# A hybrid attention decoder block: the partition swaps of the rotary tiles issued from ScalarE's queue

## The chip, the cores and the metric

The kernel runs on 1 core of one Trainium2 chip. The metric is the device time of one execution in microseconds (us). The engines are named as the profile names them: PE is TensorE (matmuls and transposes), DVE is VectorE, ACT is ScalarE, POOL is GpSimd, SP is SyncE, which does no arithmetic here and issues the DMAs. SPq and ACTq are the sequencers of SP and ACT, where a DMA instruction is issued. Each engine works through its own instructions strictly in order.

## The reference, cut to what matters

One decoder layer on 512 tokens of width 1024, all in float32: an RMS norm, one projection `h @ w_in` into queries, keys and values of two attention branches and two gates, a rotary embedding of the queries and keys, branch A (dilated window attention, 8 heads of 64), branch B (an indexer scores all keys, the best 128 of each row are kept, 8 query heads share one key head), a gated merge, an output projection, and a SwiGLU feed-forward part with a final norm. The rotary embedding is the part that the change touches:

```python
def rope(z, pos):
    half = z.shape[-1] // 2
    ...
    z1, z2 = z32[..., :half], z32[..., half:]
    return jnp.concatenate([z1 * cos - z2 * sin, z2 * cos + z1 * sin], axis=-1).astype(z.dtype)
```

Each head's 64 numbers are two halves of 32, and each half needs the other one.

## The kernel before

Every float32 operand of a matmul is split into a rounded part and a remainder (`hi`, `lo`), and a product is three matmuls (L201, L202, L203, in `mm3`). Weights come by DMA from SP into `raw` tiles (L153, five buffers), ACT copies them to `whi` (L172), and POOL or DVE makes the remainder `wlo` (L164), which also frees the `raw` buffer for the next load.

In the first quarter the kernel makes, slot by slot, the transposed queries and keys (`slot_parts`: 128 features by 512 tokens in PSUM). In that layout a head's two halves lie in different partitions, 32 apart. `rope_T` therefore copies the slot from PSUM to an SBUF tile on ACT (also named `raw`, L488, two buffers, shared tag `rp`), and swaps neighbouring blocks of 32 partitions with SBUF-to-SBUF DMAs into a tile `sw` (L491): four DMAs of 64 KB for a slot of 128 rows, two for the one with 64. `sw` is one of 39 rotating buffers (tag `k2`) that queries, keys and many other tiles share. DVE then multiplies `raw` by the cosines (L495), `sw` by the signed sines (L498), and adds (L499); ACT and DVE (L422, L426), or ACT and POOL (L441 to L447), split the sum `z` for the score matmuls. There are 13 such slots: 4 pairs of heads of branch A with 2 slots each, 4 query slots of branch B, and its keys (64 rows).

All this is laid under the attention steps of branch A. In each step (`attn_step`) two blocks go through scores on PE (L613), a masked maximum on DVE (L678), `exp` on ACT (L679), a reciprocal on DVE (L683), the normalisation on POOL (L684), transposes on PE (L693), and the split of these into `pth` on ACT (L697) and `ptl` on DVE (L698); products with the values give `y` (L708, L710), drained through `low` on ACT (L712) and added on DVE (L714). Before those, the indexer's dot products go through `relu` on ACT (L861) and a running sum `score` on DVE (L864, L866). The search for the best 128 (L629, L634, then L640 to L647) runs on DVE between all that and has to be done before branch B.

The order on PE is written out by hand. On the other engines a scheduler picks, by priority, among the instructions that are ready in its own model of time. The attention step stands at a higher priority (a lower level) than the projections under which the rotary tiles are made:

```python
        with level(2):
            tiles = qk_units([(h.q, h.k, h.half, b) for h, b in units], "sc") if units else []
            ...
        fill(us)
    def fill(us):
        debt[0] += us
        with level(3):
            while queue and debt[0] > 0:
                run_part()
```

Every DMA of the kernel is issued from SP, and ACT's queue holds no DMA.

Of the kernel before, what the change touches and what calls it, by code (L numbers as in the profile page):

```python
# [38 lines left out]
def hybrid_block(ctx: ExitStack, tc: tile.TileContext, x, norm_mix, w_in, w_up_a, w_up_b, w_out,  # L39
                 norm_ffn, w_gate, w_up, w_down, norm_final, c_rope, c_ropeT, c_mask, out):  # L40
    nc = tc.nc
# [25 lines left out]
    def k2(dt=F32, name="k2"):  # L67
        return kp.tile([P, 512], dt, tag="k2", bufs=K2, name=name)
# [261 lines left out]
    def defer(n, fn):  # L330

        if MAN[0]:
            later.append([n, fn])
        else:
            fn()
# [149 lines left out]
    def rope_T(p_, rows, then):  # L485

        raw, sw, z = kp.tile([P, 512], F32, tag="rp", bufs=2, name="raw"), k2(name="sw"), k2(name="z")
        nc.scalar.activation(raw, p_, AF.Copy)  # L488
        for i in range(rows // 32):
            o = 32 * (i ^ 1)  # L490
            nc.sync.dma_start(sw[32 * i:32 * i + 32, :], raw[o:o + 32, :])  # L491
        r = slice(0, rows)

        def straight():
            (nc.vector if RT1 else nc.gpsimd).tensor_tensor(z[r, :], raw[r, :], ropeT[r, 0, :], op=ALU.mult)  # L495

        def crossed():
            (nc.vector if RT2 else nc.gpsimd).tensor_tensor(sw[r, :], sw[r, :], ropeT[r, 1, :], op=ALU.mult)  # L498
            (nc.vector if RT3 else nc.gpsimd).tensor_tensor(z[r, :], z[r, :], sw[r, :], op=ALU.add)  # L499
            defer(1, lambda: then(z))  # L500
        defer(1, straight)
        defer(3, crossed)
        return raw
# [22 lines left out]
    def mqa_parts(res):  # L526

        ws = [stream(win, [(QB + 256 * c, 256)]) for c in range(2)] + [stream(win, [(KB, 128)], per=4)]

        def done_q(i, p_):  # L530
            rope_T(p_, P, lambda z: res.__setitem__(1 + i, queries(z, f"qB{i}")))

        def done_kv(p_):
            kv.append(rope_T(p_, HD, lambda z: res.__setitem__(0, key_twice(z, "kB"))))

        def turn_v():
            t_ = acc("vT")
            for b in range(NB):
                nc.tensor.transpose(t_[:, b * HD:(b + 1) * HD], kv[0][HALF[1], b * P:(b + 1) * P], ident[HALF[1], HALF[1]])
            v = vb()  # L540
            for b in range(NB):
                src = t_[:, b * HD:(b + 1) * HD]
                nc.scalar.activation(v[:, b, 0:64], src, AF.Copy, scale=rs1[:, b:b + 1])
                nc.vector.scalar_tensor_tensor(v[:, b, 64:128], src, rs1[:, b:b + 1],
                                               v[:, b, 0:64].bitcast(F32), op0=ALU.mult, op1=ALU.subtract)
        kv = []
        return ([slot_parts(ws[2], 0, done_kv)] +
                [slot_parts(ws[i // 2], i % 2, lambda p_, i=i: done_q(i, p_)) for i in range(4)], [(0.43, turn_v)], ws)
# [20 lines left out]
    def qka_parts(pr):  # L569
        get_w = stream(win, [(QA + P * pr, P), (KA + P * pr, P)])  # L570
        qkA[pr] = {}

        def done(m, p_):
            rope_T(p_, P, lambda z: qkA[pr].__setitem__(m, (keys if m else queries)(z, f"qk{m}A{pr}")))
        return [slot_parts(get_w, m, lambda p_, m=m: done(m, p_)) for m in range(2)], get_w
# [475 lines left out]
    for b in range(NB):  # L1051
        v = None
        for h in range(2):
            for f in range(NF - LAST, NF):
                mm3(po[b, h], (actT[f][0][:, b * P:(b + 1) * P], actT[f][1][:, b * P:(b + 1) * P]), W[f, h], False, f == NF - 1)
            o = x1[b][h]
# [53 lines left out]
```

## Time and profile before

| | us |
|---|---|
| median of 3 runs (lowest to highest) | 774.34 (773.42 to 774.81) |
| the profiled execution, its own time | 774.55 |
| its span, from the first to the last instruction | 772.8 |
| PE busy in the span | 744.1 |
| DVE busy | 435.6 |
| ACT busy | 352.6 |
| POOL busy | 281.4 |
| granted TensorE clock, as a share of full speed | 0.993 |

Busy times are means over stages that differ much: the swaps are issued from 50 to 226 us, and what counts is which engine the others wait for in that stretch. DMA-issuing instructions are not counted as busy on the engine that issues them. Matmul durations overlap, so that a stretch in which PE is 100% busy can still hold short waits.

### The profile page before, as it was taken

To read this page: it belongs to the slowest core of one execution; us is meant where nothing else is said; L and a number is where in the kernel's file an instruction comes from. 1 tells how busy PE (TensorE), PEld (TensorE's weight loads), DVE (VectorE), ACT (ScalarE), POOL (GpSimd) and SP (SyncE) were. 2 spreads that over 40 slices of the span, in tenths; PEclk is the share of its full clock that TensorE was granted. 3 is DMA by queue.
4 is the path that set the end of the run, shared out by engine and by line. 5 is a ranking of instruction groups with operands and counts; after the bars stand their busy time and mean duration, and the time that the engine had idled before them with its cause. 6 is when DMAs were issued, how large, how long until landed. Compare 5 with 4: busy or idle time off the path is not lost.

```text
span 772.8 us, 10634 instructions
## 1 busy us (share of the span) xinstructions
PE 744.1 (96%) x3621; PEld 625.2 (81%) x3621; DVE 435.6 (56%) x910; ACT 352.6 (46%) x722; POOL 281.4 (36%) x263
## 2 busy tenths in 40 slices
PE   8988998988999999999999999999999999999995
PEld 7977887886888888888887888888888888888884
DVE  5789989997766557765334344344433343222235
ACT  7366566655666667533425333333333333121233
POOL 2653656645545455422121222222222222222223
PEclk9999999999999999999999999999999999999999
DMA  8352433322432221533232332233223333323202
GB/s 278 80 137 54 102 91 88 89 76 69 117 88 70 73 66 55 176 112 107 82 106 59 109 103 88 83 109 109 84 85 105 109 101 90 105 86 109 83 14 109
DMA packets 68502, 74.53 MB, mean 96 GB/s; under 512 B 5392, under 2 KB 55584, under 8 KB 68448
## 3 DMA queue, kind: packets, MB, share of 16 engines
q1 hardware_dynamic: 68448, 73.86, 32.7%
q8 instruction: 28, 0.46, 0.2%
q14 instruction: 26, 0.21, 0.1%
HBM read 68.46 MB, written 2.10 MB: 91 GB/s over the span
## 4 chain that ended last, share of the span: by engine, by line
PE 82%; DVE 10%; ACT 3%; issue 2%; DMA 1%; SPq 0%; POOL 0%; ACTq 0%; DVEq 0%; POOLq 0%
PE o L202 5%; PE u L203 5%; PE o L203 5%; PE u L202 5%; PE u L201 5%; PE o L201 5%; PE g L203 5%; PE g L202 5%; PE g L201 5%; PE gate L201 3%; PE gate L202 3%; PE gate L203 3%; PE x L203 2%; PE x L201 2%; PE x L202 2%
## 5 line engine op out<-in xcount | busy, mean ns | idle before, releaser
L164 POOL TENSOR_TENSOR wlo<-raw,whi 128x512 fp32r<-128x512 f32 (+1 forms) x156 | 206.1, 1331 | 386.6 <-ACT whi L172 376.4
L172 ACT ACTIVATE whi<-raw 128x512 fp32r<-128x512 f32 (+1 forms) x242 | 149.6, 625 | 240.1 <-PE u L203 70.9
L164 DVE TENSOR_TENSOR wlo<-raw,whi 128x512 fp32r<-128x512 f32 x86 | 71.9, 836 | 128.3 <-ACT whi L172 127.8
L201 PE MATMUL g<-h2h,whi 128*128 128x512 f32 x176 | 68.7, 390 | 0.0
L203 PE MATMUL g<-h2l,whi 128*128 128x512 f32 x176 | 68.7, 390 | 0.0
L202 PE MATMUL g<-h2h,wlo 128*128 128x512 f32 x176 | 68.6, 390 | 0.0
L201 PE MATMUL u<-h2h,whi 128*128 128x512 f32 x176 | 68.5, 389 | 0.0
L202 PE MATMUL u<-h2h,wlo 128*128 128x512 f32 x176 | 68.5, 389 | 0.0
L203 PE MATMUL u<-h2l,whi 128*128 128x512 f32 x176 | 68.5, 389 | 0.0
L201 PE MATMUL o<-whi,ah 128*128 128x512 f32 x176 | 68.5, 389 | 0.0
L202 PE MATMUL o<-whi,al 128*128 128x512 f32 x176 | 68.5, 389 | 0.0
L203 PE MATMUL o<-wlo,ah 128*128 128x512 f32 x176 | 68.5, 389 | 0.0
L684 POOL TENSOR_SCALAR sm<-sm,st 128x256 f32<-128x256 f32 (+3 forms) x64 | 40.0, 632 | 62.4 <-DVE st L683 52.1
L201 PE MATMUL gate<-hTh,whi 128*128 128x512 f32 x128 | 51.6, 403 | 0.0
L203 PE MATMUL gate<-hTl,whi 128*128 128x512 f32 x128 | 50.2, 392 | 0.0
L202 PE MATMUL gate<-hTh,wlo 128*128 128x512 f32 x128 | 50.1, 391 | 0.0
L679 ACT ACTIVATE sm<-sm,st 128x256 f32<-128x256 f32 (+3 forms) x64 | 35.6, 557 | 23.3 <-DVE st L678 23.1
L1025 DVE TENSOR_TENSOR u<-u,rb 128x512 f32<-128x512 f32 x22 | 15.2, 692 | 52.4 <-PE u L203 52.4
L201 PE MATMUL slot<-hTh,whi 128*128 128x512 f32 x104 | 41.7, 401 | 1.8 <-DVE va L563 1.1
L201 PE MATMUL proj<-whi,hTh 128*128 128x256 f32 (+1 forms) x128 | 38.4, 301 | 2.8 <-DVE va L563 1.2
L202 PE MATMUL slot<-hTh,wlo 128*128 128x512 f32 x104 | 40.8, 392 | 0.0
L203 PE MATMUL slot<-hTl,whi 128*128 128x512 f32 x104 | 40.7, 391 | 0.0
(268 smaller groups left out, 1627.0 us busy)
## 6 DMA issues: line engine op xcount, KB each, us to landing
raw<-in_w_in SPq DMA_DIRECT2D x54, 256.0 KB, 3.0
raw<-in_w_gate SPq DMA_DIRECT2D x44, 256.0 KB, 2.9
raw<-in_w_up SPq DMA_DIRECT2D x44, 256.0 KB, 2.9
raw<-in_w_down SPq DMA_DIRECT2D x44, 256.0 KB, 2.8
x<-in_x SPq DMA_DIRECT2D x16, 256.0 KB, 4.0
raw<-in_w_in SPq DMA_DIRECT2D x32, 128.0 KB, 2.5
raw<-in_w_out SPq DMA_DIRECT2D x16, 256.0 KB, 2.6
sw<-raw SPq DMA_DIRECT2D x50, 64.0 KB, 2.0
```

Of the source, the lines that this page charges most:

```text
L164: eng.tensor_tensor(lo, raw, hi.bitcast(F32), op=ALU.subtract)
L172: nc.scalar.activation(hi, raw, AF.Copy)
L201: nc.tensor.matmul(o, l[0], r[0], start=start, stop=False)
L202: nc.tensor.matmul(o, l[1], r[0], start=False, stop=False)
L203: nc.tensor.matmul(o, l[0], r[1], start=False, stop=stop)
L679: nc.scalar.activation(sm, sm, AF.Exp, bias=st[:, 0:1], scale=-1.0, accum_out=st[:, 1:2])
L684: nc.gpsimd.tensor_scalar(sm, sm, st[:, 2:3], 1.0, op0=ALU.mult, op1=ALU.mult)
L1025: nc.vector.tensor_tensor(u, p_, rb2, op=ALU.mult)
```

## The change

The swap DMAs of `rope_T` are issued from ACT's queue in place of SP's. Their number, sizes, sources and targets stay as they are: 12 slots with four and one with two, 50 in all.

```diff
--- before.py
+++ after.py
@@ -488,7 +488,7 @@
         nc.scalar.activation(raw, p_, AF.Copy)
         for i in range(rows // 32):
             o = 32 * (i ^ 1)
-            nc.sync.dma_start(sw[32 * i:32 * i + 32, :], raw[o:o + 32, :])
+            nc.scalar.dma_start(sw[32 * i:32 * i + 32, :], raw[o:o + 32, :])
         r = slice(0, rows)
 
         def straight():
```

## Rows read from the trace of the kernel before

**Rows 1.** Busy time of each engine in three stretches of the span (us from its start): the width, PE, PE's weight loads, DVE, ACT, POOL with their instructions, the granted clock, the DMA share and GB/s.

```profile
50.00:110.00 60.00, 55.95 (x303) 48.80 (x302) 58.54 (x137) 37.60 (x77) 29.67 (x25) 0.97 0.34 84
110.00:190.00 80.00, 71.76 (x385) 60.23 (x383) 74.80 (x191) 48.13 (x110) 46.27 (x42) 0.99 0.32 82
190.00:230.00 40.00, 40.00 (x198) 33.61 (x198) 26.05 (x61) 24.58 (x57) 21.82 (x22) 0.97 0.40 105
```

**Rows 2.** Issues on SP's queue, of the swaps (L491) and of the loads of `w_in` (L153): duration in ns (lowest, median, highest), and the first and last start in us. The last line is from the page's costliest groups: ACT's copies of weights, with their count, busy us, mean ns of one, and ACT's idle time before them.

```profile
L491 SPq DMA_DIRECT2D sw<-raw x50: 507/582/1610, 50.3 to 225.7; - x50
...
L153 SPq DMA_DIRECT2D raw<-in_w_in x94: 328/373/584, 2.4 to 252.2; - x94
...
L172 ACT ACTIVATE whi<-raw 128x512 fp32r<-128x512 f32 (+1 forms) x242 | 149.6, 625 | 240.1 <-PE u L203 70.9
```

**Rows 3.** What SP's queue waited for from 48 to 230 us: in total, times, longest (us).

```profile
SPq L153 <- POOL wlo L164: 92.2, 40, 14.7
SPq L491 <- ACT whi L172: 11.4, 4, 4.1
SPq L491 <- ACT raw L488: 10.7, 4, 4.9
...
SPq L491 <- PE pT L693: 0.3, 1, 0.3
```

**Rows 4.** The two instructions of DVE's timeline that waited for a swap to land; in brackets the idle time before them and what ended it.

```profile
193.47 0.69 DVE L498 TENSOR_TENSOR sw<-sw,ropeT 128x512 f32<-128x512 f32 x1 [2.32 <-DMA sw<-raw]
...
219.38 0.97 DVE L498 TENSOR_TENSOR sw<-sw,ropeT 128x512 f32<-128x512 f32 x1 [1.40 <-DMA sw<-raw]
```

**Rows 5.** Two pieces of the chain that ended last, where it runs over a swap (its issue, and its way from issue to landing): start and length in us.

```profile
109.56 0.86 SPq L491
...
110.47 2.08 DMA sw<-raw
```

**Rows 6.** The timeline around the first two rotary slots (start, length in us, engine, line, what): ACT, SP's queue and DVE.

```profile
49.66 0.60 ACT L488 ACTIVATE raw<-slot 128x512 f32<-128x512 f32 x1 [0.19 <-PE slot L203]
50.28 2.50 SPq L491 DMA_DIRECT2D sw<-raw  x4
50.35 1.09 ACT L861 ACTIVATE relu<-dots 128x512 f32<-128x512 f32 x2
...
51.55 0.48 DVE L864 TENSOR_SCALAR score<-relu,wis 128x512 f32<-128x512 f32 x1
...
53.26 2.18 DVE L866 SCALAR_TENSOR_TENSOR score<-relu,wis,score 128x512 f32<-128x512 f32 x2 [0.38 <-ACT relu L861]
...
61.80 0.60 ACT L488 ACTIVATE raw<-slot 128x512 f32<-128x512 f32 x1
62.29 0.87 ACT L861 ACTIVATE relu<-dots 128x384 f32<-128x384 f32 x2
...
63.26 0.42 DVE L864 TENSOR_SCALAR score<-relu,wis 128x384 f32<-128x384 f32 x1
```

**Rows 7.** The timeline around the third and fourth slot: ACT and DVE.

```profile
88.96 0.58 ACT L488 ACTIVATE raw<-slot 128x512 f32<-128x512 f32 x1
...
92.86 0.60 ACT L488 ACTIVATE raw<-slot 128x512 f32<-128x512 f32 x1 [0.73 <-PE slot L203]
...
93.87 0.59 ACT L697 ACTIVATE pth<-pT 128x512 fp32r<-128x512 f32 x1
...
94.65 0.67 DVE L698 TENSOR_TENSOR ptl<-pT,pth 128x512 fp32r<-128x512 f32 x1
...
97.94 1.29 ACT L422 ACTIVATE qk0A<-z 64x512 fp32r<-64x512 f32 x2 [2.74 <-DVE z L499]
```

**Rows 8.** The timeline around the fifth and sixth slot: ACT, SP's queue and DVE.

```profile
99.47 0.60 ACT L488 ACTIVATE raw<-slot 128x512 f32<-128x512 f32 x1 [0.24 <-ACT qk0A L422]
...
109.33 3.00 SPq L491 DMA_DIRECT2D sw<-raw  x4
...
112.55 0.57 ACT L488 ACTIVATE raw<-slot 128x512 f32<-128x512 f32 x1
...
114.08 0.42 DVE L698 TENSOR_TENSOR ptl<-pT,pth 128x256 fp32r<-128x256 f32 x1 [2.42 <-ACT pth L697]
...
117.44 1.29 ACT L422 ACTIVATE qk0A<-z 64x512 fp32r<-64x512 f32 x2 [1.93 <-DVE z L499]
```

**Rows 9.** The timeline around the seventh and eighth slot, and one row behind the ninth (the slot of 64 rows): ACT and DVE.

```profile
132.55 0.58 ACT L488 ACTIVATE raw<-slot 128x512 f32<-128x512 f32 x1
...
134.13 0.59 ACT L712 ACTIVATE low<-y 64x512 f32<-64x512 f32 x1
...
134.82 0.67 DVE L714 TENSOR_TENSOR A0y<-y,low 64x512 f32<-64x512 f32 x1
...
139.81 1.29 ACT L422 ACTIVATE qk0A<-z 64x512 fp32r<-64x512 f32 x2 [2.62 <-DVE z L499]
...
141.12 0.60 ACT L488 ACTIVATE raw<-slot 128x512 f32<-128x512 f32 x1
...
144.00 0.55 DVE L698 TENSOR_TENSOR ptl<-pT,pth 128x384 fp32r<-128x384 f32 x1
...
149.42 0.63 ACT L441 ACTIVATE qk1A30h<-z 64x512 fp32r<-64x512 f32 x1 [3.80 <-DVE z L499]
...
169.78 0.63 ACT L562 ACTIVATE va<-proj,rs 128x128 fp32r<-128x128 f32 x2 [3.99 <-DVE va L563]
```

## The prediction

> **What bounds the kernel now.** I read busy time by stretch first, since the swaps lie in the first 230 us alone. From 50 to 190 us two engines are full together: DVE is busy 58.54 of 60 and 74.80 of 80 us, PE 55.95 and 71.76. From 190 to 230 us PE alone is full, 40.00 of 40, and DVE has a third of its time free [rows 1]. ACT, which is to take the issues, is busy 37.60 of 60, 48.13 of 80 and 24.58 of 40 us: it has 22, 32 and 15 us free, 69 in all. Its mean load says little, though. What matters is what stands behind a swap in ACT's order, and how soon DVE wants it.
>
> Then the waits. SP's queue stands 92.2 us for POOL's `wlo`, which frees the buffers of the weight loads, and 11.4 + 10.7 us for ACT at the swaps themselves [rows 3]. So SP has time to spare, and the loads are paced by buffers, not by the swaps. DVE waits for a swap twice, 2.32 and 1.40 us [rows 4], both times after 190 us, where it isn't full. Swaps reach DVE in time as they are.
>
> **The change part by part.**
>
> *Taken from SP.* A swap's issue takes 582 ns in the median [rows 2]; 50 of them are 29.1 us of SP's queue. Worth nothing on the path: SP waits three times as long for POOL in this stretch [rows 3], and a load issued earlier would only find its buffer still taken. If that cover were gone, SP would give back at most its waits at the swaps, 22 us of its own queue.
>
> *Landing.* Size and partitions of the transfers stay, so I keep 2.1 us from issue to landing, as in the chain [rows 5]. A swap could start sooner where SP is late: the first goes out 0.02 us after its `raw` ends (49.66 + 0.60, then 50.28 [rows 6]), but the fifth only at 109.33, 9.3 us after 99.47 + 0.60 [rows 8]. On DVE that is worth nothing as long as DVE's order is full of other work there [rows 1].
>
> *Added to ACT.* No row shows an issue on ACT. Below, it could cost nothing (if it overlapped ACT's arithmetic); above, 1.61 us, the longest on SP [rows 2]. I take SP's median: same instruction, same shape. Four in a row take 4 x 0.582 = 2.33 us, and the first slot's four took 2.50 with their gaps [rows 6]; I use the middle, 2.41 a slot. While ACT's sequencer issues, it starts no activation, and before the first it must wait for its own `raw` to be written. The 1.61 us is one extreme in 50 and is no end of the range.
>
> Two queues would now issue at once, which no row here shows. SP's load issue takes 0.373 us [rows 2]. If issues excluded each other, a slot could meet one of them: 13 x 0.373 = 4.8 us on ACT, of which, in the ratio of path to issue below (8 of 29), 1.3 us would reach the end. I leave it out. The Trainium skill (Perfetto Trace Analysis, section "DMA Instruction — HWDGE (DVE, Sync)") says that an issuing sequencer locks a shared descriptor generator for exclusive use; by that rule the sum below would be 1.3 us longer, and the change would look worse.
>
> *What is queued behind.* I take each slot twice. "Right behind": the swaps follow `raw` at once, and all that ACT does next is 2.41 us late. "Behind what is ready": ACT first does the attention work (level 2 goes before level 3), and the swaps fall into its next idle gap.
>
> - Slot 1: DVE wants the first `relu` at 51.55. Right behind, ACT is free at 50.26 + 2.41 = 52.67 and that `relu` ends at 53.2: DVE 1.7 us late. Behind the two `relu` that end at 51.44, the swaps last till 53.85, and the third `relu` ends near 54.45 for a DVE instruction that began at 53.26: 1.2 [rows 6].
> - Slot 2: right behind, 62.40 + 2.41 + 0.45 = 65.3 for DVE's 63.26: 2.0. Behind: 0 [rows 6].
> - Slots 3 and 4: right behind, 89.54 + 2.41 = 91.95, then three `whi` of 0.625 till 93.8, `raw` till 94.4, swaps till 96.8, `whi` and `pth` (0.59) till 98.0, and DVE wanted `pth` at 94.65: 3.4. Behind, the fourth slot's swaps fit into the 2.74 us before 97.94: 0 [rows 2, 7].
> - Slot 5: its swap seems held until 109.33 for another reason (below). From there 2.41 us push the work before slot 6 by about 0.6, either way [rows 8].
> - Slot 6: DVE already stands 2.42 us for `pth` at 114.08, which comes right after `raw`. Right behind: 2.4. Behind: the gap of 1.93 before 117.44 is 0.5 short [rows 8].
> - Slot 7: `low` ends at 134.72, DVE wants it at 134.82. Right behind: 2.3. Behind: 0, in the 2.62 before 139.81 [rows 9].
> - Slot 8: swaps till 141.72 + 2.41 = 144.13, `whi` and a `pth` like the others till 145.2, DVE at 144.00: 1.2. Behind: 0, in the 3.80 before 149.42 [rows 2, 7, 9].
> - Slot 9, two swaps: 0, covered by the 3.99 before 169.78 [rows 9].
> - Slots 10 to 13: 0. DVE is a third free and PE full [rows 1]; what ACT hands over goes to the next attention step, 8 us on. Without that cover, up to 2.41 each, 9.6.
>
> Right behind: 1.7 + 2.0 + 3.4 + 0.6 + 2.4 + 2.3 + 1.2 = 13.6. Behind: 1.2 + 0.6 + 0.5 = 2.3. A stall of DVE before 190 us is not made good: DVE has 1.5 us free of 60 and 5.2 of 80 [rows 1], the top-128 search has to end before branch B, and PE, full from 190 us on, starts its last 580 us that much later. Each order has something for it (SP's swap goes 0.02 us after `raw` [rows 6]; the attention step's priority in the code is higher), so I take the middle, (13.6 + 2.3)/2 = 8.0 us. The profiled execution's own time is 774.55 (span 772.8 and 1.75 around it): 782.55. It lies 0.2 above the median of the runs, so the forecast for the median is 782.3.
>
> **The rivals.**
>
> *ACT is held by the target buffer.* `sw` comes from the shared pool of 39, and a swap must wait until its buffer's last reader is done. The fifth slot's swaps wait for PE [rows 3], and the chain runs from there over a swap issued at 109.56 [rows 5], 9.5 us after `raw` was written. On SP that wait stops loads that have time; on ACT it would stop `exp`, `pth` and `whi`. If the scheduler places that swap at its `raw`, the price is up to 9.3 us more on top of the sum: 782.3 + 9.3 = 791.6. It decides from about 2 us of such a hold on, the slack of the rows above. Against it: at the other slots that I looked at closely SP waited only for ACT, so the buffer was free, and the scheduler's own model knows when a buffer comes free.
>
> *The swaps disappear into ACT's gaps.* All "behind", with an issue shorter than on SP: below 1.5 us, about 774.3 to 775.8. For it: 69 us free on ACT for 29. Against: the rows of slots 1, 2, 4, 6 and 7 leave 0.1 to 0.6 us between ACT's result and DVE's use. The Trainium skill (DMA: Bandwidth & Descriptors, "Issuing engines are not separate DMA queues") says that issuing from several engines saves sequencer time only, usually small beside the transfer; by that rule the time would stay at 774.3. The trace half agrees: 0.582 us against 2.08.
>
> *Faster.* The chain runs at 109.56 from SP's swap over its landing at 112.55 to `raw` and on to the `pth` for which DVE stands 2.42 us [rows 5, 8]. If late swaps on SP are what holds ACT's `raw` there, an own queue ends that: the 2.42 us go, 774.3 - 2.4 = 771.9. It decides where slot 5's swap can start 2.4 us earlier. Against it: ACT had no idle time before that `raw` (its row shows none), so the landing may only coincide.
>
> **How the numbers follow.** A difference under 0.2% (1.55 us) is about what a measurement of this kernel can't tell from no change. Chances: the sum, +2.3 to +13.6, 0.57; held by the buffer, 0.15; into the gaps, 0.15; faster, 0.13. Slower is the first two, 0.72; same 0.15; faster 0.13. The range runs from 772.5 (half of the faster case stays out) to 790.0 (the sum's upper bound 787.9 and a little of a hold; most of the case held by the buffer, 0.12, stays out), so that about 0.19 is left out. The forecast's own range is 776.6 to 787.9.
>
> **What would show it.** In the changed profile ACTq issues 50 swaps of about 0.58 us, and SP's waits at L491 are gone. DVE's waits for ACT (`relu`, `pth`, `raw`, `low`) before 190 us grow by some 8 us, PE's busy time in 50 to 190 us stretches over 8 us more, and after 230 us nothing changes but the start. Wrong would be: an issue on ACT of clearly other length, the swaps all behind ACT's attention work, ACT idle at a swap for DVE or PE (the buffer), a scheduler that orders DVE's instructions anew so that gains and losses lie where no swap is, or a loss after 190 us, which I put at nothing.

## The result and the profile after

The changed kernel takes 783.78 us in the median of 4 runs (783.20 to 784.11); the kernel before, run beside it, takes 773.88 (773.18 to 774.81). The ratio is 1.0126, with a 95% interval of 1.0109 to 1.0144: 9.9 us slower, where the prediction said 782.3 and slower. Its profiled execution took 783.84 us, with a span of 781.8 and a granted clock of 0.989.

The number came out close. The way to it did not, and most of what follows is about that. First the busy time by stretch, in the columns and stretches of [rows 1]:

```profile
50.00:110.00 60.00, 54.62 (x292) 46.83 (x292) 56.55 (x120) 33.43 (x72) 23.16 (x21) 0.98 0.31 78
110.00:190.00 80.00, 67.31 (x356) 57.42 (x355) 76.68 (x190) 47.10 (x104) 47.08 (x41) 0.95 0.30 77
190.00:230.00 40.00, 40.00 (x195) 33.46 (x193) 27.50 (x63) 23.27 (x56) 23.04 (x23) 0.98 0.37 95
```

From 50 to 190 us PE is busy 121.9 us and was busy 127.7 [rows 1]; the granted clock from 110 to 190 us is 0.95 and was 0.99. DVE is as full as before and ACT a little emptier. From 190 us on PE is full again. The transposes of branch B's values (L539), at the end of the stretch with the swaps, start at 221.3 us before and 230.0 after. From there to the end the two kernels run in parallel: every later matmul is 8.8 to 9.0 us late.

Now the queues. The issues of the swaps on ACT (columns as in [rows 2]), and what SP waits for from 48 to 240 us:

```profile
L491 ACTq DMA_DIRECT2D sw<-raw x50: 513/602/1594, 52.3 to 236.4; - x50
DMA to landing us min/median/max: 1.9/2.1/3.4
```

```profile
SPq L153 <- POOL wlo L164: 157.6, 46, 16.8
```

An issue takes 0.602 us on ACT and took 0.582 on SP [rows 2]; landing stays at 2.1 us; SP's waits at L491 are gone, and its time went into waiting longer for POOL, 157.6 us against 92.2 in a window that ends 10 us earlier [rows 3]. So far everything is as predicted. Then DVE's waits from 48 to 190 us, first of the kernel before, then of the changed one (engine and line, what it waited for, total, times, longest):

```profile
DVE ptl L698 <- ACT pth L697: 2.6, 2, 2.4
DVE z L495 <- ACT raw L488: 1.2, 2, 1.0
DVE score L866 <- ACT relu L861: 0.7, 2, 0.4
DVE idx L426 <- ACT idx L422: 0.5, 1, 0.5
DVE va L563 <- ACT va L562: 0.4, 1, 0.4
```

```profile
DVE ptl L698 <- ACT pth L697: 2.3, 2, 1.7
DVE score L866 <- ACT relu L861: 1.2, 2, 0.7
DVE idx L426 <- ACT idx L422: 0.7, 1, 0.7
DVE st L683 <- ACT sm L679: 0.7, 1, 0.7
DVE z L495 <- issue: 0.6, 1, 0.6
DVE score L864 <- ACT relu L861: 0.5, 1, 0.5
```

DVE waits for ACT 5.4 us before and 5.4 after (2.3 + 1.2 + 0.7 + 0.7 + 0.5). The 8 us by which these waits were to grow are not there. PE's timeline shows where the time goes instead (start, length, line, what, and in brackets the idle time before it and what ended it):

```profile
83.81 0.47 PE L201 MATMUL slot<-hTh,whi 128*128 128x512 f32 x1 [2.72 <-DVE va L563]
...
140.99 0.79 PE L201 MATMUL gate<-hTh,whi 128*128 128x512 f32 x1 [3.26 <-DVE gate L590]
...
166.65 0.35 PE L201 MATMUL proj<-whi,hTh 128*128 128x256 f32 x1 [2.77 <-DVE gate L590]
...
187.05 0.47 PE L201 MATMUL slot<-hTh,whi 128*128 128x512 f32 x1 [3.02 <-DVE va L563]
```

PE stands 11.8 us at these four places, each time for DVE, and not for rotary work: DVE has not yet emptied a PSUM accumulator of the values (`va`, L563) or of the gates (`gate`, L590) that the next projection needs. One such instruction, the first of the gates, read from all of DVE's L590 (first start and last start behind the durations), before and after:

```profile
L590 DVE TENSOR_TENSOR gate<-gate,rb x16: 667/685/692, 128.7 to 304.0; 128x512 f32<-128x512 f32 x16
```

```profile
L590 DVE TENSOR_TENSOR gate<-gate,rb x16: 661/683/692, 140.3 to 312.7; 128x512 f32<-128x512 f32 x16
```

It starts 11.6 us later, in a stretch in which PE is only some 2.6 us late. It has another place in DVE's order. The diff touches one queue, but the orders of ACT, DVE and POOL differ too, from the place on that ACT reaches at 55, DVE at 58 and POOL at 74 us of the changed kernel; only PE's, which is written out by hand, is the same. So there are two candidates: the issue time on ACT (the prediction's), and the new order that the scheduler found once the swaps were ACT's.

### The profile page after: what moved, and what is told of

Read it like the earlier page. It is cut to its first block, busy times and chain, and to the rows that moved or that the text cites. A ratio compares the mean times of both kernels' runs of the same rounds, so it can differ in the third digit from the quotient of the medians.

```text
span 781.8 us, 10604 instructions
## 1 busy us (share of the span) xinstructions
PE 748.4 (96%) x3621; PEld 629.6 (81%) x3621; DVE 441.3 (56%) x910; ACT 351.2 (45%) x722; POOL 281.6 (36%) x263
## 4 chain that ended last, share of the span: by engine, by line
PE 74%; DVE 4%; ACT 2%; issue 1%; POOL 1%; ACTq 0%; POOLq 0%; DVEq 0%
PE o L202 5%; PE u L203 5%; PE o L203 5%; PE u L202 5%; PE u L201 5%; PE o L201 5%; PE g L203 5%; PE g L202 5%; PE g L201 5%; PE gate L202 3%; PE gate L201 3%; PE gate L203 3%; PE x L202 2%; PE x L203 2%; PE x L201 2%; PE sc L613 2%
## 5 line engine op out<-in xcount | busy, mean ns | idle before, releaser
L164 POOL TENSOR_TENSOR wlo<-raw,whi 128x512 fp32r<-128x512 f32 (+1 forms) x156 | 209.1, 1350 | 374.1 <-ACT whi L172 372.8
L684 POOL TENSOR_SCALAR sm<-sm,st 128x256 f32<-128x256 f32 (+3 forms) x64 | 37.8, 597 | 86.1 <-DVE st L683 70.6
L1025 DVE TENSOR_TENSOR u<-u,rb 128x512 f32<-128x512 f32 x22 | 15.2, 692 | 52.4 <-PE u L203 52.4
```

The costliest lines, as they stand in the source:

```text
L164: eng.tensor_tensor(lo, raw, hi.bitcast(F32), op=ALU.subtract)
L684: nc.gpsimd.tensor_scalar(sm, sm, st[:, 2:3], 1.0, op0=ALU.mult, op1=ALU.mult)
L1025: nc.vector.tensor_tensor(u, p_, rb2, op=ALU.mult)
```

## The experiments

To tell them apart I held the order of chosen engines by hand. `ORDER` lists the instructions of an engine, as the scheduler of one kernel had put them, and each is tied to the one before it:

```diff
+def fix_order(tc):
+    traced = list(tc.nc.cur_bb.bb.instructions)
+    why = mybir.DependencyInfo(mybir.DependencyClass.NoSync, mybir.DependencyReason.DATA)
+    for ins in ORDER.values():
+        for a, b in zip(ins, ins[1:]):
+            tc.add_manual_dep(traced[b], traced[a].name, why, reason="order")
...
         hybrid_block(tc, *args)
+        fix_order(tc)
```

It covers the instructions from the end of the kernel's start to the end of the attention steps, and no wait is added between engines. All kernels compute the whole layer. No run holds the old order with the swaps on SP, which would show what the holding itself costs; the nearest is the mix of both orders in the table (+0.6 us). "Old order" is that of the kernel before, "new order" that of the changed one. Medians, each with the kernel before from the same chip:

| swaps issued from | order held | us | before | difference | ratio (95%) |
|---|---|---|---|---|---|
| ACT | none (the change) | 783.78 | 773.88 | +9.9 | 1.0109 to 1.0144 |
| ACT | old: ACT, DVE, POOL, SP | 780.97 | 775.05 | +5.9 | 1.0058 to 1.0088 |
| SP | new: ACT, DVE, POOL | 783.62 | 775.05 | +8.6 | 1.0093 to 1.0124 |
| ACT, highest priority | old: ACT, DVE, POOL, SP | 781.20 | 775.05 | +6.2 | 1.0066 to 1.0100 |
| ACT, highest priority | none | 788.81 | 775.05 | +13.8 | 1.0151 to 1.0193 |
| ACT for 8 slots, SP for 5 | old: all four | 777.58 | 775.13 | +2.5 | 1.0015 to 1.0039 |
| ACT | old: DVE | 783.65 | 775.13 | +8.5 | 1.0090 to 1.0133 |
| ACT | old: ACT | 785.90 | 775.13 | +10.8 | 1.0110 to 1.0170 |
| SP | new up to 66 us, then old | 775.77 | 775.13 | +0.6 | 1.0000 to 1.0025 |
| ACT | none; `va` and `gate` emptied first | 784.04 | 775.53 | +8.5 | 1.0100 to 1.0144 |
| SP | none; `va` and `gate` emptied first | 777.83 | 775.53 | +2.3 | 1.0010 to 1.0044 |
| ACT | old: ACT, DVE | 781.81 | 775.53 | +6.3 | 1.0063 to 1.0113 |
| SP | new: DVE | 778.97 | 775.53 | +3.4 | 1.0035 to 1.0077 |

**Issue alone: ACT issues, the old order held.** The edit is the change itself with `fix_order` and the old order of ACT, DVE, POOL and SP, the swaps free.

> Swaps issued from ACT, but from the end of the hand-ordered start to the end of the attention steps every other instruction of ACT, DVE, POOL and SP is held in the order of the kernel before; the swaps themselves go where the scheduler puts them. Theory 1 (the issues' own time on ACT, about 2.4 us a slot, delays what ACT hands to DVE): most of the 9.9 us stays, 779 to 784 us. Theory 2 (the issues cost little; the loss is in the new order that the scheduler gave ACT and DVE): 774 to 776 us.

+5.9 us. Here the predicted mechanism is to be seen. Of what DVE waited for from 48 to 190 us, the two largest rows:

```profile
DVE ptl L698 <- ACT pth L697: 4.5, 1, 4.5
DVE score L866 <- ACT relu L861: 2.4, 2, 1.2
```

With the smaller ones (1.1 + 1.0 + 0.6 + 0.5) DVE waits for ACT 10.1 us, 4.7 more than before. The largest wait ends at 119.86, at the sixth slot. What led to it, on ACT's timeline:

```profile
115.76 2.44 ACTq L491 DMA_DIRECT2D sw<-raw  x4
118.30 0.60 ACT L488 ACTIVATE raw<-slot 128x512 f32<-128x512 f32 x1 [1.97 <-DMA sw<-raw]
118.93 0.63 ACT L172 ACTIVATE whi<-raw 128x512 fp32r<-128x512 f32 x1
119.47 0.36 ACT L697 ACTIVATE pth<-pT 128x256 fp32r<-128x256 f32 x1
```

The fifth slot's four issues take 2.44 us; ACT stands idle 1.97 us for them; the sixth slot's `raw`, 112.55 before [rows 8], comes at 118.30. Of these 5.75 us, 3.1 are the delay that this kernel had already; the rest is about the length of the four issues, and the `pth` behind it, for which DVE already waited [rows 8], moves with it. And PE, at the transposes that need the attention step's result:

```profile
121.37 0.33 PE L693 MATMUL pT<-ident,sm 128*128 128x128 f32 x1 [1.15 <-POOL sm L684]
122.70 0.81 PE L693 MATMUL pT<-ident,sm 128*128 128x128 f32 x3 [1.00 <-POOL sm L684]
```

So a stall of ACT becomes one of DVE, then of POOL's normalisation, then of PE.

**Order alone: SP issues, the new order held.** The kernel before, with ACT, DVE and POOL in the changed kernel's order.

> The mirror: swaps issued from SP as before, but ACT, DVE and POOL held in the order of the changed kernel (ACT's order without its swaps). Theory 1 (issue time on ACT): 774 to 777 us. Theory 2 (the order): 780 to 784 us.

+8.6 us with no swap on ACT at all. PE's largest waits from 48 to 240 us are those of the changed kernel:

```profile
PE gate L201 <- DVE gate L590: 5.1, 1, 5.1
PE slot L201 <- DVE va L563: 4.7, 2, 2.7
PE proj L201 <- DVE va L563: 2.9, 1, 2.9
PE dots L613 <- ACT relu L861: 2.5, 4, 1.1
PE proj L201 <- DVE gate L590: 2.4, 1, 2.4
```

PE's order being the same, each matmul can be set against itself in the kernel before. How late it starts (us, at its time in the kernel before):

```
at              64.8   77.0   85.2  118.1  138.7  163.8  180.2  196.9
the change      -1.7   -0.3    2.6    4.3    7.5   10.2   13.4    8.8
SP, new order   -2.2   -0.8    3.6    4.7    8.9    9.7   12.9    9.2
ACT, old order   2.4    2.7    3.1    6.5    5.3    7.0    6.9    6.4
SP, new DVE     -1.7   -1.4   -0.6   -0.6    3.8    4.1    5.6    1.5
```

Each line comes from one profiled execution. The last is of one that took 776.17 us, where its three other runs took 778.85 to 779.42. The first two lines go together, within 1.5 us at each of these places. They still do when counted from 31 us, before the first swap, where the change is already 0.6 us late and the run with SP and the new order 1.6. The changed kernel's loss has the shape of the order, not that of the issues. The costs don't add: 5.9 + 8.6 would be 14.5, and the change costs 9.9. With the new order in place, what the issues on ACT add (9.9 - 8.6 = 1.3) can't be told from nothing: the two intervals, 8.4 to 11.1 us and 7.2 to 9.6, overlap.

**Where the swaps stand: highest priority, order held and free.** The swaps stand inside `with level(0)`:

```diff
-            nc.scalar.dma_start(sw[32 * i:32 * i + 32, :], raw[o:o + 32, :])
+            with level(0):
+                nc.scalar.dma_start(sw[32 * i:32 * i + 32, :], raw[o:o + 32, :])
```

> As the first of these, with the swaps at top priority, so that they go right behind their raw copy wherever their buffer is free. Theory 1: more than with the swaps at their own priority, up to the sum's bound for right behind, 778 to 788 us. Theory 2: 774 to 776 us.

> The changed kernel with its swaps at top priority and nothing else held: the scheduler orders all engines anew once more. Theory 1: the swaps still cost their issue time on ACT, 778 to 788 us. Theory 2: the time depends on the order that comes out, anywhere from 772 to 786 us.

In the old order it makes no difference that can be told from the first run (+6.2 against +5.9). That doesn't show that the place of a swap is worth nothing. The order that is held leaves little room: 30 of the 50 swaps keep their place among ACT's instructions, and 20 stand 1 to 6 instructions earlier. And the equal totals hide unequal places: at the fifth and sixth slot PE loses 0.5 us there and 4.1 in the first run, at the seventh and eighth 4.8 and 1.6 (3.2 of the 4.8 come back by 197 us).

With a free scheduler the highest priority costs 3.9 us more than the change (+13.8). PE's largest waits there are 10.2 us for `relu` and 8.2 us for the gates. Here issues and order both show. At the first two slots four swaps stand right in front of a `relu`, and PE waits 1.38 and 3.07 us for it:

```profile
51.85 2.51 ACTq L492 DMA_DIRECT2D sw<-raw  x4
54.41 1.09 ACT L862 ACTIVATE relu<-dots 128x512 f32<-128x512 f32 x2 [2.59 <-DMA sw<-raw]
...
63.91 2.45 ACTq L492 DMA_DIRECT2D sw<-raw  x4
66.46 0.87 ACT L862 ACTIVATE relu<-dots 128x384 f32<-128x384 f32 x2 [2.06 <-issue]
```

```profile
55.06 0.50 PE L614 MATMUL dots<-idx0h,idx 128*128 128x512 f32 x1 [1.38 <-ACT relu L862]
67.00 0.44 PE L614 MATMUL dots<-idx0h,idx 128*128 128x384 f32 x1 [3.07 <-ACT relu L862]
```

The longest wait for `relu`, 3.48 us at 76.53, stands 10 us behind those swaps: there ACT had waited 6.95 us for DVE. So this run shows a cost of both kinds and doesn't separate them.

**Only the slots that were costed at nothing when behind.** The old order held, slots 1, 2, 5, 6 and 8 on SP, the other eight (30 issues) on ACT:

```diff
+        slot[0] += 1
+        eng = nc.sync if slot[0] in (1, 2, 5, 6, 8) else nc.scalar
...
-            nc.scalar.dma_start(sw[32 * i:32 * i + 32, :], raw[o:o + 32, :])
+            eng.dma_start(sw[32 * i:32 * i + 32, :], raw[o:o + 32, :])
```

> The old order held on ACT, DVE, POOL and SP; the swaps of slots 3, 4, 7 and 9 to 13 (30 of the 50 issues) from ACT, those of slots 1, 2, 5, 6 and 8 from SP. Where the first run with the old order and all swaps on ACT lost time, by the start of each PE instruction against the kernel before, only those five places showed a loss that stayed. Theory a (an issue on ACT costs only where DVE or PE waits for what stands right behind it): no change, within 1.5 us of before. Theory b (each issue on ACT costs its share, 30/50 of 5.9 us): 3.5 us slower.

+2.5 by the medians, +2.1 by the ratio. That lies between the two theories, and below the 3.5 us of an equal share. In the profile the place of the loss speaks for the first theory: of the 3.0 us by which PE is late at 197 us, 0.4 are there at 31 us, and 1.5 come at 48 to 50 us, in a stretch at half the granted clock (48.2 to 51.7), while the first swap from ACT is issued at 91.5. Some 1 us is left for the eight slots. With the granted clock taken out of all runs (last section) the rest of the difference is 0.3 us.

**Which engine's order.** `fix_order` with DVE alone, with ACT alone, and with both, the swaps on ACT; and DVE alone in the new order, the swaps on SP.

> Swaps on ACT; only DVE held in the old order, ACT and POOL ordered anew by the scheduler. If DVE's new order carries the loss of the changed kernel: near the 781 us of the run with all orders held, 778 to 783 us. If ACT's new order carries it: 783 us or more.

> Swaps on ACT; only ACT (without its swaps) held in the old order, DVE and POOL ordered anew. If DVE's new order carries the loss: 783 us or more. If ACT's: 778 to 783 us.

> Swaps on ACT, with ACT and DVE both held in the order of the kernel before and POOL and SP left free. If the loss by order needs both engines' orders (DVE alone held gave 783.7, ACT alone held 785.9, all held 781.0): 780 to 782. If POOL's new order carries it: 783 to 786.

> Swaps on SP, with DVE alone held in the changed kernel's order and the other engines left free. If DVE's new order alone carries what the new order costs: 781 to 784, as with all three held in the new order (783.6). If the three orders have to come together: 774 to 778.

Holding one engine to the old order, the others free, gains little or nothing (+8.5 with DVE, +10.8 with ACT); holding both brings the time back to that of the first run (+6.3 against +5.9). These runs don't price the order of the engine that is left free, because it doesn't take the new order: with ACT held, 204 of DVE's first 470 instructions stand at their old place and 190 at their new one (compared by line and tiles), and with both held POOL comes out in the old order almost everywhere (112 of its first 114). What POOL's order is worth is thus not shown. The last run fell between its two expectations: +3.4 of the 8.6. Its PE shows the wait at the gates at the same matmul as the changed kernel:

```profile
136.31 0.80 PE L201 MATMUL gate<-hTh,whi 128*128 128x512 f32 x1 [4.57 <-DVE gate L590]
```

So the long wait for the accumulators comes with DVE's new order, though ACT and POOL have other orders here. But the wait is not yet the loss: this execution is 5.6 us late at 180 us and 1.5 at 197. The rest of the 8.6 comes only when ACT's and POOL's new orders stand with DVE's; which of the two it takes was not tried.

**Are the late accumulators a matter of priority?** The two instructions that empty them at the highest priority, in the changed kernel and, as a control, in the kernel before:

```diff
-                nc.vector.tensor_tensor(t, p_[0], rb1[0], op=ALU.mult)
+                with level(0):
+                    nc.vector.tensor_tensor(t, p_[0], rb1[0], op=ALU.mult)
```

(the same for L563).

> Swaps on ACT's queue and the scheduler free, as in the changed kernel; only the two DVE instructions that empty the accumulators of the values (L563) and of the gates (L590) get the highest priority, so that DVE does them first among what is ready. Theory A (the new order costs time because DVE empties these accumulators late and PE stands for them, 13 us of PE's waits in the changed kernel): PE's waits for va and gate shrink to 2 us or less and the time falls from 783.8 to between 776 and 781. Theory B (the order costs time in another way, and these waits only take up a delay that is there anyway): the waits move to other tiles and the time stays within 782 to 786.

> The control to the run before: swaps on SP, with the same two DVE instructions at the highest priority. Theory A: the kernel before has only short waits of PE for them, so 773 to 776. Theory B (any new order found by the scheduler is worse than the one it has, whatever changes it): 777 or more.

784.04 us with the swaps on ACT: nothing is won. For the gates the edit didn't do what it was for, since the first of them stayed where it was, at 141.3 us:

```profile
L595 DVE TENSOR_TENSOR gate<-gate,rb x16: 665/682/692, 141.3 to 314.8; 128x512 f32<-128x512 f32 x16
```

So the scheduler did not put it late for want of priority. `va`'s did come earlier (PE's waits for it fell from 7.1 to 2.3 us), and the loss came back at other tiles: 2.9 us for `sc`, 2.4 for `pT`. What held the gates in the scheduler's model stays open. Their target `t = k2(name="gate")` is one of the same 39 buffers as `sw`, so a buffer that comes free later is a candidate; it wasn't tried. The control is 2.3 us slower than the kernel before, in the range of theory B.

**A version from both.** Up to 66 us the new order leads (-1.7 in the table of delays). The new order up to that place, the old one behind it, the swaps on SP:

> Swaps from SP; ACT, DVE and POOL in the new order up to the place that PE reaches at 66 us of the kernel before, in the old order from there. Up to that place the new order was 3.9 us ahead of the old one in the run with swaps from SP, and lost from 81 us on. If the orders act place by place: 2 to 4 us faster than before, 771 to 773 us. If the early gain is taken back because DVE's other work is only put off: 774 to 776 us.

775.77 against 775.13: by the delays of the matmuls it is 3.7 us ahead at 65 us and 3.0 behind at 77, where the two orders meet. No kernel of this study beats the one before.

## Why the number was right and the way to it only half

*Right, as worked out.* The issue's length, 0.582 taken and 0.602 measured. SP's freed queue, worth nothing: it waits some 60 us longer for POOL (154.3 us up to 230 us, against 92.2). The landing, 2.1. The place: PE's stretch from 50 to 190 us grows, and behind 230 us nothing changes but the start. The direction: with the old order held, ACT's gaps, 69 us of them, do not swallow 29 us of issues.

*Right where the order is held, but as a sum and not slot by slot.* The sum was 2.3 to 13.6, taken as 8.0; the issue alone cost 5.9. By place, from the delays of the matmuls (steps between places, some of them not in the table above): the first slot 1.5 (1.2 to 1.7 forecast), the second 0.6 (0 to 2.0) and 0.8 more at 74 to 78 us, before the third, the third and fourth 0 (0 to 3.4), the fifth and sixth 4.1, of which 2.0 come back by 130 us (together 1.1 to 3.0), the seventh 0 (0 to 2.3), the eighth 1.7 (0 to 1.2), the later ones -0.5 (0). So the slot where ACT's next work was already awaited cost most, as [rows 8] said, and more than was forecast. At slots 1, 2, 3, 7 and 8 the first swap did go out 0.03 us after its `raw`, and slots 3 and 7 cost nothing even so: the terms of 3.4 and 2.3 were too high. The 1.5 us at the first slot are not shown to be the price of its issues. No wait of PE stands behind them; they are a stretch at half the granted clock that begins at 47.75 us, before the first swap is issued at 52.0, and the run with that slot on SP has it too (the changed kernel as well, below).

*Wrong in the changed kernel itself.* The step that failed is the one on which all slots were costed: that ACT, DVE and POOL keep the order of the kernel before, and the issues slide in. DVE's waits for ACT, which were to grow by 8 us, are 5.4 in both kernels. What the prediction had put under "wrong would be", an order of DVE found anew, so that losses lie where no swap is, is what happened: the new order costs 8.6 us without the change, and the issues on top of it nothing that can be told from noise. That sum and loss agree, 8.0 against 9.9, is in good part chance. That one engine's stall before 190 us can't be made good also holds less strictly than the prediction had it: the changed kernel is 13.4 us late at 180 and 8.8 at 197.

*The rivals.* "ACT held by the target buffer" did not come as a wait: the scheduler placed the swaps later instead. The fifth slot's `raw` starts at 109.37 in the changed kernel, and its swaps are issued from 117.85 on, among the attention step's `exp`. "Into the gaps" fails for all slots together; for the eight slots that were costed at nothing when behind it may hold, as their +2.1 by the ratio is mostly granted clock (last section). "Faster" had a small point: the new order does lead by 1.7 us at 65 us, and gives it back.

*The two rules.* By the rule of the shared descriptor generator (the Trainium skill, Perfetto Trace Analysis, "DMA Instruction — HWDGE (DVE, Sync)") two queues that issue side by side could lengthen each other's issues, as each waits for the lock. The rows show little of it: the median of the swaps rises by 0.02 us, and that of SP's loads of `w_in` is 0.368 and was 0.373 [rows 2], so the 1.3 us were rightly left out. The rule that several issuing engines save only sequencer time, small beside the transfer (the Trainium skill, DMA: Bandwidth & Descriptors, "Issuing engines are not separate DMA queues"), speaks of what is saved; what these runs show is the other side, 0.60 us of a sequencer that has arithmetic of its own to start, up to 5.9 us in all with the old order held.

## What to carry to other kernels

Where a scheduler orders the engines, moving a DMA to another queue is two changes, the issue time on the new engine and a new order on all engines; before pricing the first, compare the orders, and hold the old one to measure it alone. The issue itself costs most of its length (1.97 of 2.44 us at the sixth slot here) on an engine whose next instruction is already awaited, and a queue that mostly waits for buffers gains nothing by being relieved. Look at which instruction PE waits for after the change: a wait for tiles that the change never touched points to the order. But a wait need not be the loss: part of the delay can come back later.

## What the runs showed of the hardware

The clock took a share that the prediction had no term for. PE's granted clock falls to half (1.2 of 2.4 GHz) for short stretches, four in the changed kernel (columns as in [rows 1]):

```profile
48.50:51.90 3.40, 3.40 (x12) 2.72 (x11) 2.44 (x4) 1.42 (x3) 0.00 (x0) 0.50 0.85 214
140.70:144.10 3.40, 3.11 (x8) 2.53 (x9) 3.40 (x10) 3.10 (x6) 1.40 (x2) 0.50 0.10 23
168.00:171.40 3.40, 3.40 (x18) 3.40 (x17) 1.10 (x6) 2.65 (x6) 0.69 (x1) 0.50 0.14 49
188.50:191.90 3.40, 3.40 (x12) 2.85 (x11) 3.33 (x6) 2.18 (x5) 2.20 (x2) 0.50 0.30 77
```

The kernel before has two between 31 us and L539:

```profile
62.70:66.10 3.40, 3.27 (x14) 3.27 (x15) 3.37 (x5) 1.96 (x5) 2.21 (x2) 0.50 0.28 62
189.00:192.40 3.40, 3.40 (x15) 3.21 (x14) 1.54 (x7) 3.27 (x9) 3.14 (x4) 0.50 0.28 63
```

The last three of the changed kernel stand at or right behind the waits of 3.26, 2.77 and 3.02 us that end at 140.99, 166.65 and 187.05. There a wait seems to be paid twice: once as idle time, once as slow matmuls behind it. It isn't always so: behind the wait of 2.72 us that ends at 83.81 the clock stays full. Summed over all matmul records from 31 us to L539, PE is idle 15.2 us before and 21.0 after, and loses 3.4 and 6.7 us in half-clock stretches (half of its busy time there): 5.8 and 3.3 us more. Together that is 9.1 us for a stretch that grew by 8.2, so the two are right to about 1 us. With the issue alone it is 18.4 and 6.4, about half and half. The stretch near 48 us is not firmly tied to the change: it appears in this profile and in that of ACT with the old order, and not in that of SP with the new order, where the same idle time of PE stands before it. What the clock takes thus varies from profile to profile by 1 to 3 us, and times that lie closer than that say little about a single cause.

The granted clock is on record for every run, and not for the profiled ones alone: the kernel before ran at 0.985 to 0.995, in 778.86 to 772.63 us (13 runs on one chip). The span times (1 - clock) is an estimate of what the clock took in a run. It is rough, about 1 us, since it counts the low clock as lost even where PE had nothing to do. Means over all runs, each against the kernel before from the same chip (us); the change is left out, as the clocks of the runs beside it are not all on record:

| swaps issued from | order held | difference | of it clock | rest |
|---|---|---|---|---|
| ACT | old: ACT, DVE, POOL, SP | 5.7 | 2.2 | 3.5 |
| SP | new: ACT, DVE, POOL | 8.4 | 3.2 | 5.2 |
| ACT for 8 slots, SP for 5 | old: all four | 2.2 | 1.9 | 0.3 |
| ACT | old: DVE | 8.8 | 1.3 | 7.5 |
| ACT | old: ACT | 10.8 | 7.6 | 3.3 |
| ACT | old: ACT, DVE | 6.2 | 3.0 | 3.2 |
| SP | new: DVE | 3.0 | 2.8 | 0.3 |

By this estimate the rest is the same, 3.2 to 3.5 us, wherever ACT is held in the old order, with DVE held or not, and larger where it isn't and the swaps are on ACT. DVE's new order alone, and the eight slots, cost hardly anything but clock. That points to ACT's order more than to DVE's; no run holds ACT's new order alone, so it stays open.
